# A two-layer decoder trunk on one Trainium2 core: the numbers by which its list schedule is planned

## The chip, the cores and the metric

The kernel runs on one core of a Trainium2 chip. The metric is the time of the device in microseconds, the median of several executions. One further execution was taken with the hardware profiler; all rows shown here come from it.

Engines are named as in the profile: PE (TensorE, matmuls and transposes), PEld (its weight loads), DVE (VectorE), ACT (ScalarE), POOL (GpSimd) and SP (SyncE, which issues every DMA of this kernel). Each engine executes its own queue of instructions in the order in which the program issued them, and waits at an instruction until what it reads has been written and what it overwrites has been read.

## The reference

The model has 1024 tokens, a width of 1024 and two layers. Cut to what matters:

```python
for i in range(2):
    if i == 0:   # conformer convolution: x@w_in, gate, 31 taps per channel, LN, silu, @w_out
        y = conformer_conv(x, ...)
    else:        # 16 query heads on 4 shared key heads, window of 128, a sink per head
        kk, vv = shared_banded_kv(x, kv_w_k, kv_w_v, cos, sin)
        y = swa_sink_attention(x, attn_w_q, attn_sinks, attn_w_o, kk, vv, cos, sin)
    x = layer_norm(ALPHA * x + y, mix_ln_g[i], mix_ln_b[i])
    x = layer_norm(ALPHA * x + square(relu(x @ w_up[i])) @ w_down[i], mlp_ln_g[i], mlp_ln_b[i])
    x = x + (p[i] @ ple_w_proj[i]) * sigmoid(x @ ple_w_gate[i])
```

All of it is in 32-bit floats.

## The kernel before, in words

**Numbers in two halves.** TensorE multiplies a shortened 32-bit format. So each operand is split into a high half (ScalarE copies it into the short format, `h`) and a low half (VectorE subtracts, `l`), in `split` and `prep` (lines 562 and 723), and a product is three matmuls, high by high, high by low and low by high (`mm3`, line 727), of 128x128 weights by 128x512 columns into one of eight PSUM banks (tags `ps` and `tr`). The large products are done with seven block products in place of eight (Strassen's scheme in Winograd's form), whose sums VectorE forms.

**Stages, in the order of the program** (`program`, line 2190): the convolution layer (`conv`; seven channel blocks of its taps are matmuls with banded weights, one block is done on the other engines), its output and norm (`mix_out`), the MLP (`mlp`: `top_left` and pairs of up-projection blocks, then `down_seven`), the gated embedding (`ple`); then `attention` and again `mlp` and `ple`. The hidden activations and several prepared weights go to DRAM and back.

**The norm** (`layer_norm`, line 817): `stats` takes the mean and variance on VectorE (`bn_stats`, `bn_aggr`), GpSimd adds the epsilon and takes the power -1/2, VectorE makes the shift, ScalarE scales both halves of the row, VectorE multiplies by the gain, and the bias is added by `either`: VectorE or GpSimd, whichever the planner finds free. Then `to_xT` transposes the row on TensorE, and ScalarE and VectorE split it for the next product.

**What sets the order.** The functions above don't issue instructions. `Recorder.record` (line 264) notes every operation with what it depends on and with its duration from `cost` (line 311). `Recorder.schedule` (line 341) then plays the program through as a list schedule: at each step the engine that can start earliest takes, of its operations that are ready by then, the one with the lowest number (`prio`, the place in the program plus hand-set offsets such as `SOONER` and `LATE`). An operation becomes ready when the last operation that it depends on has ended, plus a latency from `delay` (line 374), plus a hand-set slack (`SLACK` 900 ns before most transposes, `UP_SLACK`, `HID_SLACK` and others). Tiles are names in pools (`SLOTS`, line 53): an allocation waits in the plan until a slot is free, which is 200 ns after the end of its last user. `both` and `held` (lines 351 to 362 and 466) make VectorE's and GpSimd's operations with two SBUF inputs exclude each other. A DMA takes SyncE for 380 ns, has one of eight lanes, and lands 4,000 ns after its issue or when the modelled traffic is through, whichever is later (lines 470 to 475). `issue` (line 482) then emits the instructions in the planned order. So all numbers in `cost` and `delay` are guesses of the planner, made in nanoseconds: they decide which instruction stands in front of which in each engine's queue, which tile gets which slot, and which engine an `either` goes to, and nothing else. How long an instruction really takes, the chip decides.

Because every instruction is emitted by `issue`, all rows of the profile have its line, L492; they are told apart by their tiles.

Of the kernel before, what the change touches and what calls it, by code (L numbers as in the profile page):

```python
# [13 lines left out]
ALU = mybir.AluOpType  # L14
# [6 lines left out]
HT = 512  # L21
# [57 lines left out]
MIX_WORK = (2, 4), (0,)  # L79
UP_NEXT = 4, 6, 0, 2  # L80
DOWN_WORK = {0: [("w_q", range(4))], 1: [("w_q", range(4, 8))], 2: [("w_o", range(4))], 3: [("w_o", range(4, 8))]}, {}
PACE = 1, 1, 2, 2, 1, 1, 1, 2, 1, 1, 1, 1, 1, 1, 1, 1
PAIRS_AHEAD = (0,), (0, 2)
GRAIN = 64
# [135 lines left out]
class Recorder:  # L220
# [90 lines left out]
    def cost(self, o, outs, allv):  # L311
        e, n = o.eng, o.name
        f = outs[0].n if outs and isinstance(outs[0], View) else 1024
        if e == "tensor":
            if n == "transpose":
                return 113.5
            return max(109.0, f * 0.4427 + 5.5 * (f < HT))
        if e == "sync":
            return 380.0
        if e == "scalar":  # L320
            t = 60.0 + f * 0.85
            if n == "activation":
                t += sum(c for k, c in (("bias", 90.0), ("scale", 130.0), ("accum_out", 110.0)) if isinstance(o.kw.get(k), View))
            return t
        if e == "gpsimd":
            if n == "tensor_tensor":
                return 460.0 if o.kw["op"] == ALU.pow else 120.0 + 2.3 * f
            return 160.0 + 1.17 * f
        psum = any(v.buf.space == "PSUM" for v in allv)
        if n == "tensor_scalar" and not psum:  # L330
            return 100.0 + f * 0.69
        if n == "bn_stats":
            return 69.0 + 1.042 * allv[-1].n
        if n == "reduce_max":
            return 70.0 + allv[-1].n * 1.042
        if n == "reciprocal":
            return 60.0 + 6.3 * f
        t = 120.0 if isinstance(o.kw.get("scalar"), View) else 70.0
        return t + f * 1.042

    def schedule(self):
        import heapq
# [10 lines left out]
        def both(o):  # L353
            if o.eng == "gpsimd":
                return o.name != "memset" and o.outv[0].n > 8
            if o.eng != "vector":
                return False
            if o.name == "tensor_copy":
                src = o.allv
            else:  # L360
                src = [v for k, v in o.kw.items() if k in ("in0", "in1") and isinstance(v, View)]
            return len(src) > 1 and not any(v.buf.space == "PSUM" for v in src)
# [5 lines left out]
        dma = 0.0  # L368
        lanes = [0.0] * 8
        order = []  # L370
        lat = 200.0
        same = dict(vector=127.0, scalar=93.0, gpsimd=100.0)

        def delay(o, x):
            a, b = o.eng, x.eng
            if a in ("alloc", "sync") or b == "alloc":
                return 0.0
            if a == b:
                return same.get(a, 0.0)
            return 200.0 if a == "tensor" else 400.0 if b == "tensor" else 240.0  # L380

        def enable(o):
            if o.eng == "alloc":
# [4 lines left out]
        def finish(o, end):  # L388
            o.end = end
            order.append(o)  # L390
            for x in o.outs:
                r = end + delay(o, x) + (0.0 if o.eng in ("tensor", "alloc") else x.slack)
                if r > x.ready:
                    x.ready = r
                x.left -= 1
                if x.left == 0:
                    enable(x)
            for b in o.bufs:
                b.users -= 1
                b.end = max(b.end, end)  # L400
                if b.users == 0 and b.slot is not None:
                    heapq.heappush(self.tags[b.tag]["free"], (b.end + lat, b.slot))
                    serve(b.tag)
# [24 lines left out]
        while True:  # L428
            best = None
            for e in engs:  # L430
                while rdy[e] and rdy[e][0][2].end:
                    heapq.heappop(rdy[e])
                while fut[e] and fut[e][0][3].end:
                    heapq.heappop(fut[e])
                if rdy[e]:
                    t = free[e]
                elif fut[e]:
                    t = max(free[e], fut[e][0][0])
                else:
                    continue  # L440
                if best is None or t < best[0]:
                    best = (t, e)
            if best is None:
                break
            t, e = best
            while fut[e] and fut[e][0][0] <= t:
                r, p, i, o = heapq.heappop(fut[e])
                if not o.end:
                    heapq.heappush(rdy[e], (p, i, o))
            p, i, o = heapq.heappop(rdy[e])  # L450
            if WAIT and fut[e] and e != "tensor":
                r, p2, i2, o2 = fut[e][0]
                if not o2.end and r <= t + WAIT and p2 < p - 300:
                    heapq.heappush(rdy[e], (p, i, o))
                    heapq.heappop(fut[e])
                    t, o = r, o2
            if o.eng == "either":
                o.eng = e
                o.dur = self.cost(o, o.outv, o.allv)
            d = o.dur  # L460
            if e == "scalar" and o.name == "activation":
                k = TABLE.get(o.args[2].name if len(o.args) > 2 else "", 0)
                if k and k != table:
                    table = k
                    d += 1283.0
            if both(o):
                d += max(0.0, held["gpsimd" if e == "vector" else "vector"] - 50.0 - t)
                held[e] = t + d
            free[e] = t + d
            if e == "sync":  # L470
                lane = max(t, lanes.pop(0))
                free[e] = lane + d
                dma = max(dma, lane + 1400.0) + max(v.transfer() for v in o.allv)
                lanes.append(max(dma, lane + 4000.0))
                finish(o, lanes[-1])
            else:
                finish(o, t + d)
# [47 lines left out]
class Emit:  # L525
# [964 lines left out]
    def mlp(self, i):  # L1490
# [90 lines left out]
        for n, cs in enumerate(DOWN):  # L1581
            self.down_seven(i, cs, n == 0, n == len(DOWN) - 1, list(range(NT)) if n == RES else [])
            nc.slack = WORK_SLACK
            for what, ks in DOWN_WORK[i].get(n, ()):
                for k in ks:
# [331 lines left out]
    def attention(self):  # L1917
# [139 lines left out]
        for h in range(2):  # L2057
            for gp in range(2):
                for m in range(2):
                    q = [heads(h, gp, m, j) for j in range(4)]  # L2060
                    for n in (4 * h + 2 * m, 4 * h + 2 * m + 1):
                        for k in range(PACE[4 * (2 * h + gp) + n % 4]):
                            if len(jobs) == 8:
# [276 lines left out]
```

## Time and profile before

| | |
|---|---|
| median of 3 executions | 2102.88 us (2102.1 to 2103.84) |
| the profiled execution, its time | 2107.08 us |
| the profiled execution, span from the first to the last instruction | 2105.0 us |
| mean clock granted to TensorE | 0.998 |
| instructions | 29324 |
| matmul and transpose instructions | 9784 |

In a row of a group, the columns after the count are the busy time in us, the mean time of one in ns, and the idle time of the engine just ahead of the group, with what ended it. In a row of stretches, each engine's busy microseconds stand with its number of instructions, then the granted clock, the share of the DMA engines and GB/s. In a timeline row the first two numbers are the start and the length of the merged row in us, and the brackets hold the idle time before it and what ended it. A busy time on TensorE is not TensorE at its peak, since matmuls overlap and their ends are modelled. The convolution layer reaches to about 400 us, its MLP and gate to about 1080, attention to about 1410, and the second MLP and gate to the end.

### The profile page before, as it was taken

To read this page: it belongs to the slowest core of one execution; us is meant where nothing else is said; L and a number is where in the kernel's file an instruction comes from. 1 tells how busy PE (TensorE), PEld (TensorE's weight loads), DVE (VectorE), ACT (ScalarE), POOL (GpSimd) and SP (SyncE) were. 2 spreads that over 40 slices of the span, in tenths; PEclk is the share of its full clock that TensorE was granted. 3 is DMA by queue.
4 is the path that set the end of the run, shared out by engine and by line. 5 is a ranking of instruction groups with operands and counts; after the bars stand their busy time and mean duration, and the time that the engine had idled before them with its cause. 6 is when DMAs were issued, how large, how long until landed. Compare 5 with 4: busy or idle time off the path is not lost.

```text
span 2105.0 us, 29324 instructions
## 1 busy us (share of the span) xinstructions
PE 2084.3 (99%) x9784; PEld 1732.3 (82%) x9784; DVE 1713.2 (81%) x2637; ACT 1204.8 (57%) x2212; POOL 309.0 (15%) x527
## 2 busy tenths in 40 slices
PE   9999999999999999999999999999999999999999
PEld 7888878888888888888878888877888888888877
DVE  7998789988875789996983677889777778888688
ACT  6767654766665644444742677656666663333374
POOL 0524023000000000001220356620000000000040
PEclk9999999999999999999999999999999999999999
DMA  6568864878876879876469686587878786575635
GB/s 225 180 203 280 285 206 155 300 249 280 273 260 212 320 256 315 275 264 230 170 198 312 231 285 211 180 299 233 273 273 277 260 284 200 180 245 167 238 120 196
DMA packets 240503, 505.16 MB, mean 240 GB/s; under 512 B 24288, under 2 KB 62944, under 8 KB 240352
## 3 DMA queue, kind: packets, MB, share of 16 engines
q1 hardware_dynamic: 240352, 503.29, 70.7%
q8 instruction: 77, 1.26, 0.2%
q14 instruction: 74, 0.61, 0.1%
HBM read 340.40 MB, written 160.17 MB: 238 GB/s over the span
## 4 chain that ended last, share of the span: by engine, by line
PE 85%; DVE 6%; DMA 4%; ACT 3%; issue 2%; POOL 1%; SPq 0%; DVEq 0%; ACTq 0%; POOLq 0%
PE ps L492 68%; PE tr L492 17%; DVE g L492 1%; ACT z L492 1%; DMA wh<-gate_t 1%; DVE t L492 1%; DVE z L492 1%; DMA raw<-in_w_up_dram 1%; DMA z<-in_w_dw_dram 1%; DVE wl L492 1%; DVE E L492 1%; DVE sm L492 0%; POOL sm L492 0%; DVE B L492 0%; DVE xl L492 0%
## 5 line engine op out<-in xcount | busy, mean ns | idle before, releaser
L492 PE MATMUL ps<-xh 128*128 128x512 f32 x618 | 240.4, 389 | 0.0
L492 PE MATMUL ps<-xl,xh 128*128 128x512 f32 x618 | 240.4, 389 | 0.0
L492 PE MATMUL ps<-xh,xl 128*128 128x512 f32 x618 | 240.4, 389 | 0.0
L492 PE MATMUL ps<-xh,wh 128*128 128x512 f32 x600 | 236.0, 395 | 3.7 <-ACT xh L492 1.5
L492 PE MATMUL ps<-xl,wh 128*128 128x512 f32 x600 | 236.1, 394 | 0.0
L492 PE MATMUL ps<-xh,wl 128*128 128x512 f32 x600 | 235.6, 393 | 0.0
L492 POOL TENSOR_SCALAR sm<-sm 128x1 f32<-128x1 f32 x72 | 26.6, 372 | 1363.7 <-DVE E L492 1201.0
L492 ACT CAST wh<-raw 128x1024 fp32r<-128x1024 f32 (+2 forms) x134 | 119.4, 894 | 90.9 <-PE ps L492 48.9
L492 PE MATMUL ps<-wh,xh 128*128 128x512 f32 (+1 forms) x424 | 166.8, 394 | 2.4 <-DVE xh L492 1.0
L492 PE MATMUL ps<-wh,xl 128*128 128x512 f32 (+1 forms) x424 | 167.2, 395 | 0.0
L492 PE MATMUL ps<-wl,xh 128*128 128x512 f32 (+1 forms) x424 | 166.9, 394 | 0.0
L492 ACT CAST xh<-wh 128x1024 fp32r<-128x1024 f32 x76 | 79.8, 1050 | 104.7 <-PE ps L492 71.2
L492 PEld LDWEIGHTS ps<-xh,wh 128*128 128x128 f32 x600 | 113.5, 189 | 27.7 <-ACT xh L492 2.0
L492 PEld LDWEIGHTS ps<-xh,xl 128*128 128x128 f32 x618 | 116.0, 188 | 24.2
L492 PEld LDWEIGHTS ps<-xl,xh 128*128 128x128 f32 x618 | 116.0, 188 | 24.2
L492 PEld LDWEIGHTS ps<-xh 128*128 128x128 f32 x618 | 116.0, 188 | 23.9
L492 ACT CAST wh<-g 128x512 fp32r<-128x512 f32 x136 | 81.3, 619 | 94.7 <-PE ps L492 53.3
L492 DVE TENSOR_TENSOR wl<-raw,wh 128x1024 fp32r<-128x1024 f32 (+2 forms) x100 | 99.7, 999 | 42.6 <-ACT wh L492 42.3
L492 PEld LDWEIGHTS ps<-xh,wl 128*128 128x128 f32 x600 | 113.4, 189 | 23.7
L492 PEld LDWEIGHTS ps<-xl,wh 128*128 128x128 f32 x600 | 113.7, 190 | 22.9 <-DVE xl L492 0.4
L492 DVE TENSOR_TENSOR wl<-g,wh 128x512 fp32r<-128x512 f32 x136 | 90.6, 690 | 43.9 <-ACT wh L492 42.8
L492 DVE TENSOR_TENSOR xl<-wh,xh 128x1024 fp32r<-128x1024 f32 x76 | 92.8, 1222 | 21.2 <-ACT xh L492 20.7
(405 smaller groups left out, 5460.3 us busy)
## 6 DMA issues: line engine op xcount, KB each, us to landing
wh<-hid SPq DMA_DIRECT2D x78, 512.0 KB, 4.7
raw<-in_w_up_dram SPq DMA_DIRECT2D x68, 512.0 KB, 4.4
wl<-in_w_down_dram SPq DMA_DIRECT2D x58, 512.0 KB, 5.0
hid<-zz SPq DMA_DIRECT2D x96, 256.0 KB, 4.6
hid<-t SPq DMA_DIRECT2D x64, 256.0 KB, 4.9
z<-in_w_dw_dram SPq DMA_DIRECT2D x56, 288.0 KB, 3.7
raw<-hid SPq DMA_DIRECT2D x30, 512.0 KB, 4.3
xh<-in_w_gate_dram SPq DMA_DIRECT2D x32, 256.0 KB, 5.5
```

What stands on the lines that cost most here:

```text
L492: getattr(getattr(nc, o.eng), o.name)(*a, **k)
```

## The change

The numbers of the planner change, and three of them get names at the top of the file. The operations, their operands, their dependencies, the offsets, the slacks and the pools stay as they are.

- In `cost`: a matmul becomes its columns plus 32 at 2.4 per ns (for 512 columns 226.7 ns as before), a transpose 109 in place of 113.5. ScalarE gets one line for PSUM operands and one for SBUF operands. GpSimd gets numbers by operation. VectorE gets a line for copies within SBUF, one for `bn_aggr`, and loses the 50 ns that a scalar operand cost.
- In `delay`: the latency to another engine was 200 ns from TensorE, 400 to TensorE, and 240 otherwise. It becomes a number of the producing engine (`seen`: 163, 95, 103 or 60) plus 300 to TensorE, or plus 100 and 34 (95 to GpSimd) to others. Between dependent operations of one engine it becomes 130 on VectorE (127), 137 on ScalarE (93) and 100 on GpSimd as before.
- In the DMA lanes: the landing is 700 ns later where the modelled traffic sets it.

```diff
--- before.py
+++ after.py
@@ -79,6 +79,9 @@
 MIX_WORK = (2, 4), (0,)
 UP_NEXT = 4, 6, 0, 2
 DOWN_WORK = {0: [("w_q", range(4))], 1: [("w_q", range(4, 8))], 2: [("w_o", range(4))], 3: [("w_o", range(4, 8))]}, {}
+TO_PE = 300.0
+MARGIN = 100.0
+LANDING = 700.0
 PACE = 1, 1, 2, 2, 1, 1, 1, 2, 1, 1, 1, 1, 1, 1, 1, 1
 PAIRS_AHEAD = (0,), (0, 2)
 GRAIN = 64
@@ -312,21 +315,27 @@
         e, n = o.eng, o.name
         f = outs[0].n if outs and isinstance(outs[0], View) else 1024
         if e == "tensor":
-            if n == "transpose":
-                return 113.5
-            return max(109.0, f * 0.4427 + 5.5 * (f < HT))
+            return 109.0 if n == "transpose" else max(109.0, (f + 32) / 2.4)
         if e == "sync":
             return 380.0
+        psum = any(v.buf.space == "PSUM" for v in allv)
         if e == "scalar":
-            t = 60.0 + f * 0.85
+            t = 40.0 + 0.85 * f if psum else 95.0 + 0.833 * f
             if n == "activation":
-                t += sum(c for k, c in (("bias", 90.0), ("scale", 130.0), ("accum_out", 110.0)) if isinstance(o.kw.get(k), View))
+                t += sum(c for k, c in (("bias", 90.0), ("scale", 95.0), ("accum_out", 96.0)) if isinstance(o.kw.get(k), View))
             return t
         if e == "gpsimd":
             if n == "tensor_tensor":
-                return 460.0 if o.kw["op"] == ALU.pow else 120.0 + 2.3 * f
-            return 160.0 + 1.17 * f
-        psum = any(v.buf.space == "PSUM" for v in allv)
+                return 545.0 if f == 1 else 100.0 + 2.95 * f
+            if n == "memset":
+                return 85.0 + 0.82 * f
+            if n == "affine_select":
+                return 60.0 + 1.1 * f
+            if n == "tensor_copy":
+                return 120.0 + f
+            return 272.0 if f <= 8 else 170.0 + 1.3 * f
+        if n == "tensor_copy" and not psum:
+            return 65.0 + 0.52 * f
         if n == "tensor_scalar" and not psum:
             return 100.0 + f * 0.69
         if n == "bn_stats":
@@ -335,8 +344,9 @@
             return 70.0 + allv[-1].n * 1.042
         if n == "reciprocal":
             return 60.0 + 6.3 * f
-        t = 120.0 if isinstance(o.kw.get("scalar"), View) else 70.0
-        return t + f * 1.042
+        if n == "bn_aggr":
+            return 118.0
+        return 66.0 + f * 1.042
 
     def schedule(self):
         import heapq
@@ -369,7 +379,8 @@
         lanes = [0.0] * 8
         order = []
         lat = 200.0
-        same = dict(vector=127.0, scalar=93.0, gpsimd=100.0)
+        same = dict(vector=130.0, scalar=137.0, gpsimd=100.0)
+        seen = dict(tensor=163.0, vector=95.0, scalar=103.0, gpsimd=60.0)
 
         def delay(o, x):
             a, b = o.eng, x.eng
@@ -377,7 +388,7 @@
                 return 0.0
             if a == b:
                 return same.get(a, 0.0)
-            return 200.0 if a == "tensor" else 400.0 if b == "tensor" else 240.0
+            return seen[a] + (TO_PE if b == "tensor" else MARGIN + (95.0 if b == "gpsimd" else 34.0))
 
         def enable(o):
             if o.eng == "alloc":
@@ -471,7 +482,7 @@
                 lane = max(t, lanes.pop(0))
                 free[e] = lane + d
                 dma = max(dma, lane + 1400.0) + max(v.transfer() for v in o.allv)
-                lanes.append(max(dma, lane + 4000.0))
+                lanes.append(max(dma + LANDING, lane + 4000.0))
                 finish(o, lanes[-1])
             else:
                 finish(o, t + d)
```

## The prediction

> **What bounds the kernel now.** I read the page's busy times first, then stretches, then TensorE's waits, then the handover where most is lost. The change reorders instructions only, so the question is how much of the span an order can give back.
>
> ```profile
> span 2105.0 us, 29324 instructions
> PE 2084.3 (99%) x9784; PEld 1732.3 (82%) x9784; DVE 1713.2 (81%) x2637; ACT 1204.8 (57%) x2212; POOL 309.0 (15%) x527
> ...
> 15.00:150.00 135.00, 134.61 (x701) 115.09 (x701) 125.54 (x185) 95.06 (x173) 38.59 (x47) 1.00 0.63 200
> 500.00:950.00 450.00, 450.00 (x1987) 372.62 (x1986) 370.86 (x510) 241.12 (x362) 0.00 (x0) 1.00 0.80 272
> 1500.00:2000.00 500.00, 500.00 (x2208) 414.01 (x2207) 392.42 (x539) 248.20 (x368) 0.00 (x0) 1.00 0.70 238
> 2050.00:2105.00 55.00, 50.53 (x234) 41.83 (x232) 46.05 (x73) 22.86 (x38) 4.55 (x3) 1.00 0.60 203
> ...
> 568.17 27.20 PE ps L492 x120
> ```
>
> TensorE is idle for 2105.0 - 2084.3 = 20.7 us. In a run of 120 matmuls on the chain one takes 27.20/120 = 0.227 us. In 500 to 950 there is one per 450/1987 = 0.226, in 1500 to 2000 one per 500/2208 = 0.226: the MLP stretches, 950 us, lose nothing. The work is unchanged, so nothing can be won there. The rest is convolution, gates and attention. The last stretch holds 55 - 50.53 = 4.5 us idle, the tail after the last matmul included.
>
> ```profile
> 1.51 2.07 PE L492 MATMUL ps<-t 128*128 128x512 f32 x4 [1.51 <-DVE t L492]
> ...
> 2100.60 0.28 PE L492 MATMUL ps<-wh,xl 128*128 128x256 f32 x1
> ```
>
> Idle time understates: a matmul is shown for 0.39 us but the next may start after 0.227, so a wait hides up to 0.16 more. Between these first and last rows lie 9,784 starts. Summing each start's delay beyond the median distance of its pair of shapes, where over 20 ns, I get 44.7 us in 275 places. That is the ceiling: not below 2102.9 - 44.7 = 2058.
>
> ```profile
> PE ps L492 <- POOL B L492: 2.4, 2, 1.6
> PE ps L492 <- ACT t L492: 1.4, 3, 0.6
> PE tr L492 <- DMA wh<-gate_t: 1.1, 1, 1.1
> PE tr L492 <- ACT X L492: 0.7, 1, 0.7
> PE ps L492 <- DVE xl L492: 0.5, 1, 0.5
> PE tr L492 <- ACT t L492: 0.4, 1, 0.4
> PE ps L492 <- ACT A L492: 0.4, 1, 0.4
> PE ps L492 <- DMA wh<-gate_t: 0.3, 1, 0.3
> PE ps L492 <- DMA B<-scr: 0.2, 1, 0.2
> ```
>
> These waits (total, times, longest) end with an engine or a transfer whose planned time the change moves.
>
> **The change part by part.** Nothing is added or removed; each planned number moves towards or away from what was recorded. I test that at the last layer norm of attention, the costliest handover.
>
> ```profile
> 1396.67 1.07 ACT L492 CAST xh<-ps 128x512 fp32r<-128x512 f32 x2
> 1397.28 1.29 DVE L492 TENSOR_TENSOR xl<-ps,xh 128x512 fp32r<-128x512 f32 x2 [1.38 <-ACT xh L492]
> 1398.48 0.20 DVE L492 BATCH_NORM_AGGREGATE sm<-sm 128x2 f32<-128x12 f32 x1
> 1398.60 0.63 DVE L492 SCALAR_TENSOR_TENSOR B<-B,ps 128x512 f32<-128x512 f32 x1
> 1398.77 0.19 POOL L492 TENSOR_SCALAR sm<-sm 128x1 f32<-128x1 f32 x1 [5.82 <-DVE sm L492]
> 1399.04 0.55 POOL L492 TENSOR_TENSOR sm<-sm,mhalf 128x1 f32<-128x1 f32 x1
> 1399.94 1.52 ACT L492 ACTIVATE z<-B,sm 128x512 f32<-128x512 f32 x2 [0.77 <-DVE sm L492]
> 1401.02 0.20 DVE L492 BATCH_NORM_AGGREGATE sm<-sm 128x2 f32<-128x12 f32 x1
> 1402.75 3.12 POOL L492 TENSOR_TENSOR B<-z,g 128x512 f32<-128x512 f32 x2
> 1402.89 1.24 DVE L492 SCALAR_TENSOR_TENSOR sm<-sm,sm 128x1 f32<-128x1 f32 x1
> 1404.17 0.81 ACT L492 ACTIVATE z<-B,sm 128x512 f32<-128x512 f32 x1 [2.20 <-DVE sm L492]
> 1408.20 0.66 PE L492 MATMUL ps<-ident,B 128*128 128x128 f32 x4 [1.62 <-POOL B L492]
> 1408.89 0.59 ACT L492 CAST xh<-ps 128x512 fp32r<-128x512 f32 x1 [1.69 <-PE ps L492]
> ```
>
> *Times.* The plan's cost of an operation is the distance from its start to the next one's. ScalarE from PSUM: two casts end after 1.07 and one is shown for 0.59, so they start 0.48 apart; old 0.495, new 0.475. VectorE from PSUM: two end after 1.29 and one is shown for 0.68 (the rows under D), so 0.61; old 0.604, new 0.600. The aggregate: 1398.60 - 1398.48 = 0.12; old 0.072, new 0.118. GpSimd's one-column step: 1399.04 - 1398.77 = 0.27; old 0.161, new 0.272. Its power: 0.55; old 0.460, new 0.545. Its 512-column add: 3.12/2 = 1.56; old 1.298, new 1.610. So the large errors were GpSimd's, and they go.
>
> *Latencies.* TensorE to VectorE or ScalarE goes from 0.200 to 0.163 + 0.1 + 0.034 = 0.297. Four transposes starting at 1408.20 reach the cast at 1408.89: 0.69. Old: 4 x 0.1135 + 0.200 = 0.654; new: 0.436 + 0.297 = 0.733. The one is 0.04 short, the other 0.04 long; the new errs on the safe side. To TensorE nearly nothing moves (0.400 to 0.395 and 0.403).
>
> *The norm's chain*, aggregate to scaling: recorded 1399.94 - 1398.48 = 1.46; planned 1.634 before and 1.815 now (118+290+272+100+545+194+67+229). The next one, beside GpSimd's adds, took 1404.17 - 1401.02 = 3.15: both plans are short, the new by 1.3.
>
> *Who does the add.* The second row of each norm's end may go to VectorE or to GpSimd: the plan takes whichever can start first, whatever the add costs there. GpSimd being busy 0.312 longer for each, an add may pass to VectorE (0.60 there); between none and all 30 (rows under E), worth from nothing to 1.0 each where the add is late. I take nothing: the first add of a norm finds GpSimd idle either way.
>
> *Queues.* Every engine runs its queue in plan order, SyncE's too: an issue stays 0.38, and what moves is which load stands first. Behind an instruction that waits, all of its engine's queue waits; on TensorE that is the loss counted above, on ScalarE (57% busy) and GpSimd (15%) it is mostly covered.
>
> *Landings.* The plan lands a transfer 4.0 us after its issue, or later where the modelled traffic queues, and there 0.7 is added. The transfer of the two gate waits:
>
> ```profile
> wh<-gate_t SPq DMA_DIRECT2D x16, 512.0 KB, 6.7
> ```
>
> It takes 6.7, so 0.7 is in the right direction; it also moves no DMA's work, only which consumers are ordered ahead.
>
> *The sum.* An order that knows the truth puts ready work ahead of what would wait. The quoted waits sum to 2.4+1.4+1.1+0.7+0.5+0.4+0.4+0.3+0.2 = 7.4 us idle, in 12 places that hide up to 12 x 0.16 = 1.9 more. And behind the 1.62 us wait the clock falls:
>
> ```profile
> 1409.00:1412.00 3.00, 2.65 (x8) 2.26 (x9) 3.00 (x5) 1.69 (x3) 0.00 (x0) 0.54 1.03 383
> ```
>
> Granted 0.54 costs 2.65 x 0.46 = 1.2. Together 10.5. Of it I leave the 1.3 of the disturbed norm and the clock's 1.2, since a wait that only shrinks may still lower it: 8.0 stays. Unknown is what other waits the new order makes: from below nothing, or even a further gain (VectorE's waits go too), from above the rivals' 12. I take zero, as the longest stretches show that TensorE mostly has ready work. The profiled execution took 2107.08 for its span of 2105.0, and the median is 2102.88, 4.2 lower; the waits are absolute, so 2102.9 - 8.0 = 2095.
>
> The Trainium skill (TensorE: Matmul & The Clock Gate, "What's actually happening") says that TensorE falls to half rate after at least one idle window of about 3.4 us. Here 0.54 was granted after single waits of at most 1.62 us, so the trace speaks against the need of one whole window. By the rule no wait here touches the clock and the sum is 8.0; by the row, were the wait to go wholly, it is 9.2 and the time 2094, and each new wait of this size costs 1.2 more than its length.
>
> **The rivals.** (A) The forecast, 2095.
>
> (B) The small delays and VectorE's waits go as well: two fifths of the 44.7, so 2102.9 - 18 = 2085. For it: the VectorE row agrees to 0.01 us. Against: these costs hardly moved, so the order around them has little cause to.
>
> (C) The order changes only where TensorE has work anyway: 2103. For it, the 950 us that lose nothing; against, the twelve places above.
>
> (D) Slower: the longer TensorE latency. In the plan a PSUM result is ready 0.097 later; where VectorE comes free inside that time the plan gives it a weight's low half instead, and the PSUM bank is freed that much later. Place: convolution and attention, where VectorE is busy 125.54 of 135.
>
> ```profile
> L492 DVE TENSOR_TENSOR wl<-raw,wh 128x1024 fp32r<-128x1024 f32 x58 | 72.0, 1244 | 16.4 <-ACT wh L492 16.1
> L492 DVE TENSOR_TENSOR B<-B,ps 128x512 f32<-128x512 f32 x96 | 65.3, 682 | 22.6 <-PE ps L492 22.4
> L492 DVE TENSOR_TENSOR t<-t,ps 128x512 f32<-128x512 f32 x77 | 52.6, 683 | 25.1 <-PE ps L492 19.1 <-ACT t L492 5.6
> L492 DVE TENSOR_TENSOR E<-E,ps 128x512 f32<-128x512 f32 x63 | 42.9, 682 | 3.3 <-PE ps L492 3.1
> ```
>
> 96+77+63 = 236 such adds; a window of 0.097 against a split of 1.24 turns some 8% of them, 19. Half reaching TensorE at 1.24 is 12 us: 2115; all, 2126. It decides from the point where the delayed evacuation finds no other free bank: then TensorE's next product stands at the head of its queue, and all behind it. Where a bank is free it costs nothing. For it: the slacks written by hand (0.9 before most transposes) stay and add to the same side; against it, in the MLP stretches no bank is ever waited for.
>
> (E) GpSimd's recorded time holds waiting for VectorE already, and the plan makes the two exclude each other on top.
>
> ```profile
> L492 POOL TENSOR_TENSOR B<-z,g x3: 1368/1647/1789, 1402.8 to 1406.5; 128x512 f32<-128x512 f32 x3
> ...
> L492 POOL TENSOR_TENSOR E<-z,g 128x512 f32<-128x512 f32 x16 | 25.7, 1619 | 4.8 <-DVE z L492 3.8 <-issue 1.0
> L492 POOL TENSOR_TENSOR B<-z,g 128x512 f32<-128x512 f32 x14 | 21.5, 1545 | 14.9 <-DVE z L492 9.0 <-issue 3.4 <-PE ps L492 2.5
> ```
>
> The shortest, 1.368, lies near the old 1.298; a 0.15 us step of VectorE took 1.24 beside it. If all 30 adds push a norm's end back in the plan by 0.312, 9.4 us of order is wrong, two thirds on the path: 2109. The Trainium skill (GPSIMD Engine Reference, "8. Key points") says that GpSimd shares its SBUF interfaces with VectorE and contends with instructions of two SBUF inputs; the 1.24 agrees.
>
> **How the numbers follow.** A 0.44, B 0.11, C 0.12, D 0.24, E 0.09. Forecast 2095. Within 0.2% (4.2 us, about what a measurement of this kernel can tell from no change) is C: 0.12; faster A and B, 0.55; slower D and E, 0.33. A alone spans 2088 to 2098. As both signs hold much, the range reaches from half of the ceiling, 2081, to just past D, 2116, leaving about 0.1 on each side.
>
> **What would show it.** Right: the same counts of instructions on each engine; TensorE's idle time down from 20.7 to about 13; the POOL wait before the transposes at the end of attention and the 0.54 gone; 500 to 950 and 1500 to 2000 unchanged. (B): VectorE's waits gone too. (D): new waits of TensorE in the convolution and attention for VectorE, with a weight's split just before the add. (E): new waits around the norms. Wrong altogether: a loss inside the MLP, or GpSimd given markedly fewer adds.

## The result and the profile after

The changed kernel takes 2109.50 us (median of 13 runs, 2104.41 to 2112.43), the kernel before 2102.85 us (13 runs, 2101.59 to 2108.12). The ratio is 1.0026, with a 95% interval of 1.0017 to 1.0034: slower by a quarter of a per cent, where 8 us faster was forecast.

The page of the changed kernel, its first lines, and then its stretches (length; busy microseconds and instructions of PE, PEld, DVE, ACT and POOL; granted clock, share of the DMA engines, GB/s):

```profile
span 2106.5 us, 29368 instructions
## 1 busy us (share of the span) xinstructions
PE 2084.0 (99%) x9784; PEld 1732.8 (82%) x9784; DVE 1708.4 (81%) x2635; ACT 1207.6 (57%) x2212; POOL 310.8 (15%) x529
...
150.00:200.00 50.00, 49.54 (x284) 43.06 (x284) 42.68 (x58) 37.77 (x75) 27.47 (x38) 1.00 0.85 262
...
260.00:290.00 30.00, 26.05 (x138) 21.54 (x139) 28.08 (x52) 23.41 (x46) 13.41 (x14) 1.00 0.68 233
...
500.00:950.00 450.00, 450.00 (x1987) 372.59 (x1987) 372.00 (x512) 244.60 (x366) 0.00 (x0) 1.00 0.81 273
...
1400.00:1415.00 15.00, 11.69 (x46) 8.91 (x45) 9.81 (x16) 6.74 (x13) 6.17 (x4) 0.77 0.93 302
...
1500.00:2000.00 500.00, 500.00 (x2208) 414.01 (x2207) 391.76 (x539) 249.15 (x368) 0.15 (x1) 1.00 0.70 235
...
2050.00:2107.00 57.00, 50.06 (x230) 41.14 (x228) 47.13 (x76) 23.37 (x38) 5.08 (x3) 1.00 0.65 217
```

The same stretches of the kernel before, where they were not shown above:

```profile
150.00:200.00 50.00, 47.57 (x264) 40.57 (x263) 44.19 (x58) 38.44 (x75) 26.92 (x39) 1.00 0.83 269
...
260.00:290.00 30.00, 28.53 (x156) 23.29 (x155) 28.97 (x60) 25.15 (x51) 15.29 (x23) 1.00 0.83 287
...
1400.00:1415.00 15.00, 12.11 (x53) 9.55 (x52) 14.36 (x22) 7.70 (x13) 6.13 (x5) 0.89 0.93 325
```

The work is the same: 9,784 matmuls and transposes, and on balance two operations that went from VectorE to GpSimd (2637 to 2635, 527 to 529), which the groups of GpSimd show to be adds. TensorE's idle time goes from 20.7 to 2106.5 - 2084.0 = 22.5 us. The MLP stretches are as they were, and nothing is lost in them. Elsewhere the idle time moved: 2.4 down to 0.5 us in 150 to 200, but 1.5 up to 4.0 us in 260 to 290 (the norm after the taps), and at the end of attention 2.9 up to 3.3 us with a lower clock, 0.77 in place of 0.89. After 2050, where the last gate is, it goes from 4.5 to 6.4 us (2106.5 - 2050 - 50.06).

What TensorE waited for in the changed kernel (total us, times, longest):

```profile
PE ps L503 <- issue: 3.1, 2, 2.1
PE ps L503 <- POOL B L503: 2.9, 2, 2.3
PE tr L503 <- POOL A L503: 1.8, 1, 1.8
PE ps L503 <- DMA wh<-gate_t: 1.6, 3, 1.1
...
PE ps L503 <- DMA wh<-form: 1.0, 1, 1.0
PE tr L503 <- ACT t L503: 1.0, 1, 1.0
...
PE ps L503 <- ACT A L503: 0.9, 1, 0.9
PE ps L503 <- ACT t L503: 0.5, 1, 0.5
```

Of the 7.4 us of waits that the forecast meant to remove, 2.6 are gone. The others stand at the same handovers and have grown from 4.9 to 7.3 us: GpSimd's adds at the end of attention, ScalarE's `t` at two places of the convolution layer, the gates' transfers, and ScalarE's `A` near 1310. Beside them there are new ones. Three handovers can be followed further, the first two to their cause.

*The end of attention.* GpSimd, VectorE, then TensorE, around the last norm:

```profile
1399.04 5.90 POOL L503 TENSOR_TENSOR B<-z,g 128x512 f32<-128x512 f32 x3 [1.55 <-DVE z L503]
1404.90 1.27 POOL L503 TENSOR_TENSOR B<-v,g 128x512 f32<-128x512 f32 x1
...
1399.04 3.45 POOL L503 TENSOR_TENSOR B<-z,g 128x512 f32<-128x512 f32 x1 [1.55 <-DVE z L503]
...
1398.27 1.89 DVE L503 TENSOR_TENSOR z<-z,g 128x512 f32<-128x512 f32 x3
1400.08 0.68 DVE L503 TENSOR_TENSOR v<-v,g 128x512 f32<-128x512 f32 x1
1400.68 0.68 DVE L503 TENSOR_TENSOR X<-X,X 128x512 fp32r<-128x512 f32 x1
1403.86 0.69 DVE L503 TENSOR_TENSOR xl<-ps,xh 128x512 fp32r<-128x512 f32 x1 [2.49 <-ACT xh L503]
...
1402.54 0.66 PE L503 MATMUL ps<-ident,B 128*128 128x128 f32 x4 [2.31 <-POOL B L503]
1403.77 0.79 PE L503 MATMUL ps<-ident,B 128*128 128x128 f32 x4 [0.56 <-POOL B L503]
1404.99 1.12 PE L503 MATMUL tr<-ident,B 128*128 128x128 f32 x4 [0.44 <-POOL B L503]
```

The third row is the first of the three adds by itself. The largest wait, 2.31 us, ended when this add ended, at 1399.04 + 3.45 = 1402.49. An add of this size takes 1.26 to 1.30 us when VectorE has no two-input work in SBUF beside it (the section on the hardware has the count). Here VectorE had four such operations in a row beside it (the last two `z<-z,g`, `v<-v,g` and `X<-X,X`), up to 1400.68 + 0.68 = 1401.36, and the add ended 1.13 us after the last of them.

All four bias adds of the last two rows of the norm now stand in GpSimd's queue, one behind the other, 5.90 + 1.27 us. Before, VectorE had done the last one. Who gets such an add is settled in the plan, by who is free first there. But no start of TensorE waited for the end of this fourth add at 1406.17: the three waits of 2.31, 0.56 and 0.44 us ended with the first three.

The waits also cost clock. The lower clock is 0.50, for 6.8 us from 1404.2 in the changed kernel and for 3.4 us from 1409.2 before; the first row is of the changed kernel, the second of the kernel before:

```profile
1404.30:1411.00 6.70, 6.26 (x20) 4.78 (x19) 4.27 (x7) 1.98 (x4) 1.87 (x2) 0.50 0.93 323
...
1409.30:1412.60 3.30, 3.25 (x10) 2.69 (x11) 3.30 (x5) 1.39 (x3) 0.00 (x0) 0.50 1.03 385
```

*The norm after the taps.* GpSimd's scaling, VectorE beside it, then the transposes that need it:

```profile
L503 POOL TENSOR_SCALAR A<-A,sm x8: 767/771/4985, 255.9 to 278.9; 128x512 f32<-128x512 f32 x8
...
278.87 4.99 POOL L503 TENSOR_SCALAR A<-A,sm 128x512 f32<-128x512 f32 x1 [2.70 <-issue]
...
279.68 3.70 DVE L503 TENSOR_TENSOR E<-E,bo 128x512 f32<-128x512 f32 x6
...
283.91 0.55 PE L503 MATMUL tr<-ident,A 128*128 128x128 f32 x3 [1.81 <-POOL A L503]
...
L492 POOL TENSOR_SCALAR A<-A,sm x8: 769/1030/1922, 261.0 to 281.2; 128x512 f32<-128x512 f32 x8
```

One of eight equal scalings took 4.99 us in place of 0.77. Six adds of VectorE with two SBUF inputs ran through in the same 4 us, and the scaling ended just after the last of them (279.68 + 3.70 = 283.38; 278.87 + 4.99 = 283.86). In the order before (the last row), the longest of the eight took 1.92. The plan counts every operation of GpSimd of more than 8 columns, except `memset`, as excluding VectorE's two-input ones, this scaling too (`both`), and there the two take turns; on the chip GpSimd got no turn for six adds.

*The last gate.* ScalarE's cast of a weight, two reads of PSUM by VectorE, then TensorE's next load and product (the longer of the two waits listed under "issue"):

```profile
2074.90 1.04 ACT L503 CAST wh<-raw 128x1024 fp32r<-128x1024 f32 x1 [2.17 <-PE tr L503]
...
2076.18 1.29 DVE L503 TENSOR_TENSOR zz<-zz,ps 128x512 f32<-128x512 f32 x2
...
2076.94 0.19 PEld L503 LDWEIGHTS ps<-wh,xh 128*128 128x128 f32 x1 [2.50 <-ACT wh L503]
2076.97 0.47 PE L503 MATMUL ps<-wh,xh 128*128 128x512 f32 x1 [2.11 <-issue]
```

The cast waits until TensorE has finished with the tile it overwrites, and ends at 2074.90 + 1.04 = 2075.94. The load, which the trace puts down to this cast, starts only 1.0 us later, and what held it for this time the trace does not tell. The first of VectorE's two reads of PSUM ends at 2076.87, just before it, so a bank that came free then is a candidate; this is not shown. In the order before, a cast of this form ran at 2075.66 while TensorE still had products of the gate in its queue.

Summed as in the prediction, the delays of TensorE's starts come to 46.3 us after, against 44.7 before; span less delays is 2060.2 against 2060.3. So the delays are the whole difference between the two traces. But this is 1.6 us, and the ratio of 1.0026 means 5.5. The profiled execution of before took 2107.08, 4.2 over its median, that of after 2108.53, 1.0 under its own. One trace of each cannot show the other 4 us. The granted clock has a part in the 5.5. The 13 executions of the changed kernel were granted 0.9978 on average, 137 of the kernel before on five other chips 0.9990, and its profiled one 0.998. Among those 137, the executions at 0.998 took 2105.3 us on average, those at 0.999 2103.7 and those at 1.000 2102.0. At 1.7 us for 0.001, about 2 of the 5.5 us go with the clock (an estimate from these numbers; the two traces hold a part of it already).

### The profile page after: what moved, and what is told of

Its sections match the earlier page's. It is cut to its first block, busy times and chain, and to the rows that moved or that the text cites. A ratio compares the mean times of both kernels' runs of the same rounds, so it can differ in the third digit from the quotient of the medians.

```text
span 2106.5 us, 29368 instructions
## 1 busy us (share of the span) xinstructions
PE 2084.0 (99%) x9784; PEld 1732.8 (82%) x9784; DVE 1708.4 (81%) x2635; ACT 1207.6 (57%) x2212; POOL 310.8 (15%) x529
## 3 DMA queue, kind: packets, MB, share of 16 engines
q8 instruction: 77, 1.26, 0.2%
## 4 chain that ended last, share of the span: by engine, by line
PE 93%; DMA 3%; DVE 1%; ACT 1%; issue 1%; POOL 0%; SPq 0%; DVEq 0%; POOLq 0%; ACTq 0%
PE ps L503 75%; PE tr L503 18%; DMA wh<-gate_t 1%; DMA raw<-in_w_up_dram 1%; DMA raw<-in_w_out_dram 0%; DMA wh<-form 0%; SPq L503 0%; DVE wl L503 0%; DMA z<-in_w_dw_dram 0%; ACT wh L503 0%; DMA raw<-in_w_o_dram 0%; DMA X<-in_xT_dram 0%; POOL A L503 0%; DMA A<-in_w_up_dram 0%; DVE t L503 0%
## 5 line engine op out<-in xcount | busy, mean ns | idle before, releaser
L503 PE MATMUL ps<-xh,wh 128*128 128x512 f32 x616 | 241.3, 394 | 1.3 <-ACT t L503 0.5
L503 PE MATMUL ps<-xl,wh 128*128 128x512 f32 x616 | 241.9, 393 | 0.2 <-DVE xl L503 0.2
L503 PE MATMUL ps<-xh,wl 128*128 128x512 f32 x616 | 241.1, 392 | 0.0
L503 PE MATMUL ps<-wh,xh 128*128 128x512 f32 x408 | 162.7, 400 | 5.9 <-issue 3.1
L503 PE MATMUL ps<-wl,xh 128*128 128x512 f32 x408 | 161.9, 397 | 0.0
L503 PE MATMUL ps<-wh,xl 128*128 128x512 f32 x408 | 161.4, 396 | 0.0
```

Source lines behind the costliest of these rows:

```text
L503: getattr(getattr(nc, o.eng), o.name)(*a, **k)
```

## The experiments

Three theories stood against each other. **Theory 1**, rival D of the prediction: the longer latencies are to blame. **Theory 2**: the change redraws the whole order, and any redrawing moves the time by a few microseconds either way, whichever number causes it. **Theory 3**, rival E: GpSimd's new times are to blame. Each ratio below is to the kernel before on the same chip, with its 95% interval.

**The three parts alone**, each put into the kernel before, and one redrawing by a number that the change leaves alone.

`e1_costs`: only the new `cost`.

> The kernel before with the new operation times alone. Theory 1 (the longer latencies make the changed kernel slow): this part holds the gain, so 3 to 8 us faster than before. Theory 2 (any redrawn order moves the time, whichever part redraws it): somewhere between 6 us faster and 10 us slower, not tied to the part, and the three parts' differences don't sum to the 5 to 7 us of the whole.

2107.84 us, ratio 1.0019 (1.0010 to 1.0028): slower by about 4 us, where theory 1 saw the gain.

`e2_latency`: only the new `delay`.

```diff
-        same = dict(vector=127.0, scalar=93.0, gpsimd=100.0)
+        same = dict(vector=130.0, scalar=137.0, gpsimd=100.0)
+        seen = dict(tensor=163.0, vector=95.0, scalar=103.0, gpsimd=60.0)
...
-            return 200.0 if a == "tensor" else 400.0 if b == "tensor" else 240.0
+            return seen[a] + (TO_PE if b == "tensor" else MARGIN + (95.0 if b == "gpsimd" else 34.0))
```

> The kernel before with the new latencies alone. Theory 1: slower than before by 7 us or more, with TensorE's waits for VectorE and ScalarE in convolution and attention. Theory 2: between 6 us faster and 10 us slower.

2098.93 us, ratio 0.9982 (0.9973 to 0.9991): faster by about 4 us. Theory 1 falls: the latencies alone make no loss.

`e3_landing`: only `max(dma + LANDING, ...)`.

> The kernel before with the landing 700 ns later alone. Theory 1: within 3 us of before. Theory 2: between 6 us faster and 10 us slower, as far off as the others although it is the smallest of the three parts.

2105.09 us, ratio 1.0007 (0.9998 to 1.0017): no difference that can be told, and not the size that theory 2 wanted.

`e4_slot220`: that number, the time after which a slot counts as free, 20 ns up.

```diff
-        lat = 200.0
+        lat = 220.0
```

> The kernel before with one number of the plan that the change does not touch moved by 20 ns (a slot counts as free 220 ns after its last user in place of 200), so a redrawn order with no meaning. Theory 1: within 2 us of before. Theory 2: off by 3 us or more, to either side, about as far as the change.

2104.93 us, ratio 1.0002 (0.9993 to 1.0011). This draw speaks against theory 2, which wanted 3 us or more. The three parts sum to +0.19 - 0.18 + 0.07 = +0.08%, the whole is +0.26%.

**The operation times divided by engine, and the change without them.**

`e5_gpsimd`: only GpSimd's lines of `cost`.

> The kernel before with the new times of GpSimd alone. Theory 3 (GpSimd's recorded times already hold its waits for VectorE and the plan adds the exclusion again): this part carries the loss of the operation times, so 3 us or more slower than before. Theory 2 (any redrawn order moves the time by a few us, whichever part): between 4 us faster and 5 us slower, and the three parts of the times don't sum to their whole (plus 4.0).

2111.31 us (5 executions), ratio 1.0035 (1.0023 to 1.0048): slower by 7 us, as theory 3 wanted, and more than theory 2 allowed.

`e5_scalar`: only ScalarE's lines.

> The kernel before with the new times of ScalarE alone. Theory 3: within 2 us of before. Theory 2: between 4 us faster and 5 us slower.

2108.14 us, ratio 1.0021 (1.0011 to 1.0030): slower by 4 us, where theory 3 wanted at most 2.

`e5_vector`: only VectorE's and TensorE's lines.

> The kernel before with the new times of VectorE and TensorE alone (the smallest corrections: 4 to 5 ns, 46 for one small operation, 50 for those with a scalar operand). Theory 3: within 2 us of before. Theory 2: between 4 us faster and 5 us slower, as far off as the large corrections.

2106.15 us, ratio 1.0007 (0.9998 to 1.0016): within what theory 3 wanted. The three engines' parts sum to 0.35 + 0.21 + 0.07 = 0.63%, yet together they made 0.19%: the parts don't add.

`e6_latland`: latencies and landing, with the old `cost`.

> The changed kernel without its operation times (the new latencies and the later landing stay). If the parts add: minus 3.8 from the latencies and plus 1.5 from the landing, so 2 to 3 us faster than before, and the operation times are what makes the change slow. Theory 2: the parts don't add, and it may be off from that by 3 us or more to either side.

2096.41 us (5 executions), ratio 0.9963 (0.9949 to 0.9976): faster by 8 us than before and by 13 than the changed kernel. It beats both kernels, by more than the 2 to 3 us of the added parts. Its page and TensorE's waits:

```profile
span 2093.7 us, 29308 instructions
...
PE ps L496 <- DVE t L496: 2.4, 2, 1.5
PE ps L496 <- POOL B L496: 1.9, 2, 1.6
PE ps L496 <- DMA wl<-form: 1.4, 2, 0.9
PE ps L496 <- DMA wh<-gate_t: 1.3, 2, 1.1
```

The wait for GpSimd's scaling is not there, those for its adds are 1.9 in place of 2.9, and the delays of TensorE's starts sum to 33.1 us; 2093.7 - 33.1 = 2060.6, as for the others. So the gain too is in the waits, and the clock stayed at 1.00 until the end.

**GpSimd's old times put back into the changed kernel.**

`e7_after_oldgp`: all of GpSimd's old lines.

> The changed kernel with GpSimd's old times. Theory 3 (GpSimd's new times carry the loss): 5 us or more faster than the changed kernel, about the time of before or under it. Theory 2 (redrawn orders, no part is to blame): anywhere from 8 us faster to 4 us slower than the changed kernel, and not at the same places.

2103.08 us, ratio 1.0001 (0.9992 to 1.0010), 5 us under the changed kernel, as theory 3 wanted.

`e7_after_oldadd`: only the add's old line.

```diff
-                return 545.0 if f == 1 else 100.0 + 2.95 * f
+                return 545.0 if f == 1 else 120.0 + 2.3 * f
```

> The changed kernel with the old time of GpSimd's add alone (1.298 in place of 1.610 us for 512 columns); its other new times stay. Theory 3 in the form of rival E (the recorded add holds waits for VectorE that the plan adds again): as good as with all of GpSimd's old times, 5 us or more faster than the changed kernel. If GpSimd's small steps (norm's chain) are what matters: within 2 us of the changed kernel.

2105.49 us, ratio 1.0009 (1.0000 to 1.0018): 4 us under the changed kernel, between the two expectations.

**The good and the bad order redrawn.**

`e8_latland_slot220` and `e8_after_slot220`: `lat = 220.0` in `e6_latland` and in the changed kernel.

> The kernel with the new latencies and landing but the old operation times (2096.4 us), its order redrawn by the number without meaning (a slot counts as free after 220 ns in place of 200). If the latencies' gain is of the model: 2096 plus or minus 3. Theory 2 (a lucky draw): back to 2100 or more.

> The changed kernel with its order redrawn in the same way. If the loss is of the model's numbers: within 3 us of the changed kernel, 2106 to 2112. Theory 2 (an unlucky draw): under 2105.

The first takes 2105.06 us, ratio 1.0005 (0.9996 to 1.0014): the gain of 0.37% is gone. The second takes 2105.01 us, ratio 1.0008 (0.9999 to 1.0017): two thirds of the loss are gone. Twenty nanoseconds in a number that the change leaves alone moved one by 9 us up and the other by 4 down. With this, theory 2 leads, and the good record of theory 3 is in doubt: an engine's lines redraw the order as well.

**Two more draws of each of the three models**, with slots of 180 and of 210 ns.

> Before, redrawn (slot time 180 ns). Theory 2 (each order is a draw around a common middle): between 2098 and 2111. If the model sets the time: 2101 to 2105, as at 200 and 220.

> The changed kernel, redrawn (slot time 180 ns). Theory 2: between 2098 and 2111. If the refitted numbers are worse in themselves: over 2105.5, and the four draws' mean 3 us or more above that of before.

> New latencies and landing with the old operation times, redrawn (slot time 180 ns). Theory 2: between 2098 and 2111. If the latencies and landing are better in themselves: under 2100, and the four draws' mean 3 us or more below that of before.

> Before, redrawn (slot time 210 ns). Theory 2 (each order is a draw around a common middle): between 2098 and 2111. If the model sets the time: 2101 to 2105.

> The changed kernel, redrawn (slot time 210 ns). Theory 2: between 2098 and 2111. If the refitted numbers are worse in themselves: over 2105.5.

> New latencies and landing with the old operation times, redrawn (slot time 210 ns). Theory 2: between 2098 and 2111. If the latencies and landing are better in themselves: under 2100.

Medians, and ratios to before with their intervals, of all twelve:

| slot free after | old numbers | new latencies and landing | all new numbers |
|---|---|---|---|
| 180 ns | 2107.22, 1.0015 (1.0006 to 1.0024) | 2101.15, 0.9988 (0.9979 to 0.9997) | 2108.55, 1.0023 (1.0014 to 1.0032) |
| 200 ns | before: 2102.85, 1 | 2096.41, 0.9963 (0.9949 to 0.9976) | the change: 2109.50, 1.0026 (1.0017 to 1.0034) |
| 210 ns | 2103.57, 1.0002 (0.9993 to 1.0011) | 2103.95, 1.0004 (0.9995 to 1.0013) | 2099.54, 0.9985 (0.9976 to 0.9993) |
| 220 ns | 2104.93, 1.0002 (0.9993 to 1.0011) | 2105.06, 1.0005 (0.9996 to 1.0014) | 2105.01, 1.0008 (0.9999 to 1.0017) |
| mean of the ratios | 1.0005 | 0.9990 | 1.0011 |

Within one model the draws lie up to 0.42% apart (0.9963 to 1.0005), more than the change makes. The four draws of the old numbers lie closer, 0.15% apart. Singly, the changed model at 180 ns (2108.55) is where a worse model should be, and at 210 ns (2099.54) it is not. The all-new model is the slower by 0.35% than its partial form at 180 ns and the faster by 0.19% at 210. Its mean is 0.06% above that of the old numbers, 1.2 us, where the expectation for a worse model asked for 3; with a scatter of about 0.19% in each of the two new models a mean of four is uncertain by 0.1%. So the loss of this change is of the size of a draw, and that the refitted model is worse, or better, is not shown.

In the good draw of the changed model, 210 ns, GpSimd's and VectorE's adds of the last norm stand like this:

```profile
1395.03 2.21 POOL L503 TENSOR_TENSOR B<-z,g 128x512 f32<-128x512 f32 x1 [2.26 <-DVE z L503]
1397.87 3.34 POOL L503 TENSOR_TENSOR B<-z,g 128x512 f32<-128x512 f32 x2 [0.63 <-DVE z L503]
...
1400.71 1.04 DVE L503 TENSOR_TENSOR B<-v,g 128x512 f32<-128x512 f32 x1
```

All planned times and latencies are those of the changed kernel. VectorE has the last add again. What counts for TensorE is the first: it took 2.21 us in place of 3.45 and ended at 1397.24, while TensorE still had products to do, up to the transposes of that row at 1398.84, which start without a wait. GpSimd is in none of TensorE's waits over 0.15 us in this trace.

## Why the prediction was wrong

**The bound** held. TensorE is the bound, the MLP loses nothing in either order, and the differences are TensorE's delays. In all twenty kept traces the span less these delays is 2059.4 to 2061.1 us, at spans of 2093.7 to 2109.7. The delays include the starts that a lower clock spaces out.

**The refit's accuracy** held for the operations shown, with one exception that the section on the hardware takes up: GpSimd's add. That the chip then waits less did not follow.

**The sum.** Its working was a list of waits to be removed, 10.5 us, 8.0 of them counted. In the changed kernel they are mostly still there: for the adds on GpSimd 2.4 became 2.9 + 0.4, for the gates' transfers 1.4 became 1.6, for ScalarE's `t`, `X` and `A` 2.9 became 2.4. Those that stayed at their handovers grew from 4.9 to 7.3 us.

**The step that failed** is this one: "Unknown is what other waits the new order makes [...] I take zero, as the longest stretches show that TensorE mostly has ready work". The longest stretches are those that don't matter. In the stretches that do, the new order made 1.8 us for the scaling, 3.1 in two waits that the trace gives to no engine and 1.0 for a prepared weight, and from 1400 to 1415 it was granted 0.77 of the clock in place of 0.89. A planned order is not the old one with its errors taken out: it is another order, and it has waits of its own.

**Who does the add** was named and taken at nothing, "the first add of a norm finds GpSimd idle either way". At the last norm of attention the first add did find GpSimd idle (1.55 us before it), and the add that moved, the fourth, ended no wait of TensorE; so nothing was the right price for the move here. What had no term is the time of the first add itself, 3.45 us beside VectorE, which is behind the largest wait, 2.31 us.

**Rival D** (longer latencies) is refuted as told: alone they gained 0.18%. **Rival E** was the nearest in time, 2109, which alone is no evidence for its mechanism. Its sign, new waits around the norms, is there too. GpSimd's times alone lose 0.35%, and putting the old ones back gains 5 us; but ScalarE's alone lose 0.21%, and a slot time of 210 ns gains 9 us with GpSimd's new times in place. TensorE's waits for GpSimd sum to 0 to 5.1 us, 3.3 on average, in the six traces with all of GpSimd's new times, and to 1.0 to 3.6, 2.5 on average, in the thirteen with none of them; these overlap too much to decide, and a scaling of 4.38 us stands in `e5_scalar` as well, with GpSimd's old times. Its mechanism remains possible and is not shown. **Rival C** ("the order changes only where TensorE has work anyway") fails on the new waits above: the order changed where TensorE had no other work, too.

**The range.** The stated range, 2081 to 2116, holds the 2109.5, and the eighteen experiments too, from 2096 to 2111; but the change is on the other side of no change. What was missing was a rival for the redrawing itself: a scatter of 0.2% around no change in either direction, without a mechanism of its own.

What stays open: most of the 4 us by which the medians differ more than the two traces, what held TensorE in the last gate, and whether over many draws one of the models is better by 0.1% or so.

## What to carry to other kernels

When a planner orders the work and the bounding engine is at 98% (2060 of 2105 us here), a change of the plan's numbers is a new draw before it is an improvement: redraw it by a small step in some other number, several times, before believing a gain or a loss of 0.2%. Keep the best order that was found for what it is, an order (here 2096.4 us), and expect that the next edit loses it. At the two handovers that could be followed here it was not an operation's mean time that the plan had wrong, but how long one engine is held out by another; look at the waits behind what two engines share.

## What the runs showed of the hardware

GpSimd can be held out by VectorE over many instructions, not one: a scaling that takes 0.77 us alone took 4.99 during six adds of VectorE in a row. The twenty kept traces hold 160 such scalings. The 89 that had no two-input work beside them (less than 0.05 us of VectorE's `tensor_tensor` with both inputs in SBUF) took 0.76 to 1.08 us. The five longest, 4.38 to 4.99 us in five different orders, had 3.88 to 4.57 us of it beside them. The Trainium skill (GPSIMD Engine Reference, "8. Key points") says that the two share SBUF interfaces and contend there; the traces agree, and here the difference was 4.2 us.

GpSimd's add of 512 columns has no one time either, as two groups of the changed kernel show:

```profile
L503 POOL TENSOR_TENSOR B<-B,t 128x512 f32<-128x512 f32 x3 | 3.9, 1292 | 13.2 <-DVE t L503 13.2
...
L503 POOL TENSOR_TENSOR E<-v,g 128x512 f32<-128x512 f32 x2 | 3.5, 1738 | 0.0
```

Of the 853 such adds in the twenty traces, the 122 with no two-input work beside them took 1.26 to 1.30 us, the other 731 took 1.27 to 3.45, half of them between 1.61 and 1.74. The old number of the plan, 1.298, is that of an add alone. The refitted 1.610 lies between the kinds: of the 42 adds of the changed kernel 12 took 1.26 to 1.31, 8 took 1.58 to 1.65 and 20 took 1.68 to 1.83.

TensorE's clock fell again without a pause of several microseconds: three waits of 2.31, 0.56 and 0.44 us at the end of attention left 0.77 granted in 1400 to 1415. The Trainium skill (TensorE: Matmul & The Clock Gate, "What's actually happening") gives about 3.4 us of idleness for that; the longest single wait here is 2.31 us, their sum 3.31.

The traces show how much idleness was enough. Within the span the clock record holds 1.00 and 0.50 alone, and 0.50 comes in pieces of 3.41 us or two or three of them. Eighteen of the traces have such a fall before 2085 us; cut into pieces that begin and end with the falls, they give 30 pieces at full clock just before a fall, and in each of them TensorE, by its records in the trace, stood idle for 1.50 to 2.92 us, in one wait or in several. In the 10,922 pieces at full clock after which the clock stayed, it was at most 1.81 us. So about half a piece was enough here.
